# A rotation table for all state-space batches, the gate's token sums in a lane of their own, and new lane paces

## The chip, the cores and the metric

The kernel runs on one core of one Trainium2 chip. Its time is the device time of one execution in microseconds (us). The core's engines each take their instructions in a fixed order and wait for one another by semaphores: TensorE (PE: matmuls, with PEld for its weight loads), VectorE (DVE), ScalarE (ACT), GpSimd (POOL) and SyncE (SP), which here only issues DMA transfers.

## The reference

The reference is one layer of a decoder block with two token mixers side by side, in float32, for 1024 positions and 16 meta tokens put ahead of them, with 1024 features:

```
h     = layer_norm(concat(meta, x))
p     = h @ w_in + b_in            # columns: u_s5 | q | k | v | o | i | f | g_s5 | g_m
z     = gelu(S5(u_s5)) @ w_glu     # S5: 32 groups of 16 channels, 64 complex states each
y_s5  = z[:, :1024] * sigmoid(z[:, 1024:])
y_m   = (sigmoid(o) * head_norm(mLSTM(silu(conv(q)), silu(conv(k)), v, i, f))) @ m_w_out
mix   = sigmoid(g_s5) * y_s5 + sigmoid(g_m) * y_m
h     = layer_norm(ALPHA * h + mix @ w_o)
h     = layer_norm(ALPHA * h + square(relu(h @ w_up + b_up)) @ w_down)
```

The mLSTM is a gated linear attention with four heads; S5 is a linear recurrence per channel group. The output leaves the meta tokens out.

## The kernel before

**Split products.** Every large matrix product is made of three passes on PE: each operand is split into a rounded half (ACT copies it to the rounded type: `whi`, `hT_hi`, `gelh`) and the rest (DVE subtracts: `wlo`, `hT_lo`, `gell`). mm3 (L222 to L228) issues hi x hi (L226), lo x hi (L227) and hi x lo (L228). A product therefore waits for ACT's `whi` (L212, and L1042 in the Strassen part) first and for DVE's `wlo` (L213, L1043) right after.

**Jobs and lanes.** After the first layer norm the projection is cut into jobs of 128 output features, in the order of ORDER: q (queries and keys), v, o, u (the S5 input), g (the S5 gate), m (the other gate), and then z0 to z7 for the GLU product (`z2s`, `sgs`, L944 and L945 add up its parts). Each job loads its weights two jobs ahead, splits them, and runs its matmuls. Everything else is written as Python generators in lanes: `ml` (mLSTM), `cv` (convolution), `s5`, `s5c`, `s5g` (state space), `ah` (the residual and early FFN work). A job that emits matmuls calls pump(dt) with its own length, and each lane then emits its next piece whenever its clock has come; the number that a generator yields is the pause until its next piece. A scheduler turns the emitted program into a fixed order for each engine; PE's work, DVE's, ACT's and the DMA queue are then run in that order, each instruction waiting for its operands and for its tile's slot. Nearly all tiles come from one ring of 30 slots of 4 KB per partition (`slot`).

**State space.** s5_pre (L579) computes the discretised constants for all groups; it is added to lane `s5c` at job S5_START. Then, for each of four batches of 8 groups, s5_consts (L674) makes the batch's matrices (`s5P`, `s5Mi`, `s5Kt`, `s5Rr`, `s5Ri`, `s5Mx`; POOL copies blocks by small DMAs) and its rotation table `s5T`, powers 0 to 129 of a complex rotation for 4 columns, built by doubling: eight levels of six DVE operations (cmul, L572 to L577). s5_batch (L790) uses them: products `s5z` and `s5y` on PE, rotations `s5w` on DVE, and s5_gelu (L866) applies the gelu (`gelf`, `gelh`, `gell`). The tables ML, NL, C5, K5, Z5, D5, W5 and Y5 hold the pauses of these generators for each of the four heads or batches.

**Early residual and FFN work.** ah_scale (L1369) scales the residual rows. up_early (L1400) prepares the first three (PRE) pairs of FFN weight blocks for the later Winograd product: for each pair it loads two blocks (`wur`), makes four sums (`wus`, L1394 to L1397), splits seven blocks (`wpre`, L1412 on ACT and L1413 on DVE), and stores each to memory (`wu_dr`, L1414). Both are added to lane `ah` at job g4.

**The gates and the mLSTM output.** Next to the m gate and the mLSTM output product comes the class Seven: seven Strassen products over blocks of weights and of tokens. The token blocks are `rawb`, loaded by raw_block, and the sums of token blocks are made by sub (L1000 to L1002). begin() loads four blocks at job z7; after the last job all lanes are drained, and first() splits the first weights and makes the sums:

```
for l in lanes.values():
    l.drain()
first()
run7()
```

After that come the output projection with its layer norm, the FFN up and down products and the tail. They aren't touched.

Of the kernel before, what the change touches and what calls it, by code (L numbers as in the profile page):

```python
# [9 lines left out]
F32 = mybir.dt.float32  # L10
F32R = mybir.dt.float32r
I32 = mybir.dt.int32
AF = mybir.ActivationFunctionType
OP = mybir.AluOpType
P = 128
# [4 lines left out]
META = 16  # L20
# [20 lines left out]
ORDER = "q0 q1 v0 q2 v1 q3 o1 o0 v2 o2 o3 u0 u1 v3 u2 g0 u3 g1 o4 o5 o7 o6 g2 g3 g5 g6 g4 g7 m0 m1"  # L41
S5_START = "u0"
NM = 2
SPLIT_UP = 200
PRE = 3
ZD = 1
ML = [2.4, 1.2, 1.68, 4.8]
NL = [0.88, 1.75, 1.75, 1.75]
C5 = [0.7, 0.98, 1.96, 0.49]
K5 = [1.7, 3.4, 1.7, 1.7]  # L50
Z5 = [1.0, 1.0, 1.0, 1.0]
D5 = [2.88, 1.22, 1.44, 1.44]
W5 = [2.21, 1.56, 2.6, 2.6]
Y5 = [1.97, 2.82, 3.38, 2.82]
AFT = 0
VAFT = 2
LOAD0 = "x0 x1 w0 c0 x2 w1 c1 x3 x4 w2 x5 w3 x6"
# [55 lines left out]
def decoder_block(  # L113
# [4 lines left out]
    nc = tc.nc  # L118
    v_, a_, g_, t_ = nc.vector, nc.scalar, nc.gpsimd, nc.tensor
# [9 lines left out]
    def slot(name, dt=F32):  # L129
        return big.tile([P, SLOT], dt, tag="s", name=name)  # L130
# [12 lines left out]

    lanes = {"ml": Lane(), "cv": Lane(), "s5": Lane(), "s5c": Lane(), "s5g": Lane(), "ah": Lane()}
    clock = [0.0]
# [48 lines left out]
    def load_w(job):  # L194
        job.raw = []
        for src, n in job.loads:
            r = slot("wraw") if ring[0] is None else ring[0].tile([P, 1024], F32, tag="wr", bufs=3, name="wraw")
            nc.sync.dma_start(r[:, :n], src)
            job.raw.append(r)
# [379 lines left out]
    def s5_pre():  # L579
# [14 lines left out]
        S5["ni"] = mid.tile([P, 16], I32, name="s5_ni")  # L594
        yield 1.3
        lr, li = lam[:, 0], lam[:, 1]
# [5 lines left out]
        acc_exp(ea, a, (t1, t2))  # L602
        yield 1.3
        r8 = t16("r8")
# [11 lines left out]
        a_.activation(cs, t1, AF.Sin, scale=-1.0, bias=hpi_t[:, 0:1])  # L616
        yield 1.3
        es = slot("s5E")
# [12 lines left out]
        for _ in range(3):  # L631
# [3 lines left out]
            v_.tensor_tensor(p8[:, 0], t1, t2, op=OP.subtract)  # L635
        yield 1.3
        for n in (1, 2, 4):
# [4 lines left out]
                 E[:, 0, n:n + 1].to_broadcast(sh), E[:, 1, n:n + 1].to_broadcast(sh), w1, w2)  # L642
        yield 1.3
        for j in range(8):
# [14 lines left out]
        v_.tensor_tensor(wi, wi, inv, op=OP.mult)  # L659
        yield 1.3  # L660
        sh = [P, 16, 16]

        def v3(ap):
# [5 lines left out]
             v3(tm[:, 0:256]), v3(tm[:, 256:512]))  # L669
        yield 1.3  # L670

    GEL = {}

    def s5_consts(b):  # L674
# [85 lines left out]
        yield K5[b]  # L760
        T = slot("s5T")
        tc_, ts_ = (T[:, i * 520:(i + 1) * 520].rearrange("p (q c) -> p q c", q=4) for i in range(2))
        tmp = slot("s5tt")
        g_.memset(tc_[:, :, 0], 1.0)
        g_.memset(ts_[:, :, 0], 0.0)
        g_.tensor_copy(tc_[:, :, 1], S5["p8"][:, 0, q0:q0 + 4])
        g_.tensor_copy(ts_[:, :, 1], S5["p8"][:, 1, q0:q0 + 4])
        yield C5[b]
        n = 1
        while n < 129:  # L770
            m = min(n, 129 - n)
            sh = [P, 4, m]
            w1 = tmp[:, 0:4 * m].rearrange("p (q c) -> p q c", q=4)
            w2 = tmp[:, 512:512 + 4 * m].rearrange("p (q c) -> p q c", q=4)
            cmul(v_, tc_[:, :, n + 1:n + 1 + m], ts_[:, :, n + 1:n + 1 + m], tc_[:, :, 1:m + 1], ts_[:, :, 1:m + 1],
                 tc_[:, :, n:n + 1].to_broadcast(sh), ts_[:, :, n:n + 1].to_broadcast(sh), w1, w2)
            n *= 2
            yield C5[b]
        S5["m", b] = (RS, Mi, Mx, T)

# [204 lines left out]

    def raw_block(dr, kh, ch, off=0):
        ts = [slot("rawb"), slot("rawb")]
        for i in range(2):
            k = 4 * kh + 2 * i
            c = off + 512 * ch  # L990
            tc.keep_in_program_order(nc.sync.dma_start(s3(ts[i]), dr[k:k + 2, :, c:c + 512].rearrange("k p s -> p k s")))  # L991
        return ts
# [7 lines left out]
    def sub(dst, a, b):  # L1000
        for i in range(2):
            v_.tensor_tensor(dst[i][:, :1024], a[i][:, :1024], b[i][:, :1024], op=OP.subtract)  # L1002

    class Seven:
# [8 lines left out]
        def load(self, i):  # L1013
            if i >= self.ntile():
                return
            r = ring[0].tile([P, 1024], F32, tag="wr", bufs=3, name="wraw")
            for j, (n, p) in enumerate(self.units[2 * i:2 * i + 2]):
                s = {5: 0, 6: 1, 7: 2, 3: 3}.get(n)
                if s is None:
                    t = self.w[self.i0 + 2 * p + (n == 4)].rearrange("p k f -> p (k f)")  # L1020
                    a = t[:, 0:512] if n == 1 else t[:, 512:1024]
                else:
                    a = ws_dr[self.p0 + p, s]
                tc.keep_in_program_order(nc.sync.dma_start(r[:, j * 512:j * 512 + 512], a))
            self.raw[i] = r
# [117 lines left out]
    def gates_and_output():  # L1143
        h00, h10, h01, h11 = home(0, 0), home(1, 0), home(0, 1), home(1, 1)
        g = Seven(3, wf, JGM + NM, 0, {1: h00, 2: h10, 6: h01, 7: h00, 4: h10, 5: h01, 3: h11})
        y = Seven(4, wmo, 0, 3, {1: h00, 2: h10, 6: h01, 7: h11, 4: h00, 5: h10, 3: h01})
        R, M = {}, {}

        def begin():
            for nm, kh, ch in (("12", 0, 1), ("22", 1, 1), ("11", 0, 0), ("21", 1, 0)):  # L1150
                R[nm] = raw_block(h_dr, kh, ch, META)

        def first():
            for i in range(3):
                g.load(i)
            g.split(0)
            sub(R["22"], R["12"], R["22"])
            sub(R["12"], R["12"], R["11"])
            sub(R["11"], R["11"], R["22"])
            to_home(R["11"], h01)  # L1160
            sub(R["21"], R["21"], R["11"])
            R.pop("11")

        def hm_load():
            for nm, kh, ch in (("11", 0, 0), ("12", 0, 1), ("22", 1, 1), ("21", 1, 0)):
                M[nm] = raw_block(hm_dr, kh, ch)

        def y_start():
            for i in range(3):
                y.load(i)  # L1170
            y.split(0)
        ghooks = {1: [lambda: to_home(R.pop("22"), h00)],
                  2: [lambda: to_home(R.pop("21"), h10)],
                  6: [lambda: to_home(R.pop("12"), h01), hm_load],
                  7: [lambda: to_home(M["11"], h00), lambda: sub(M["12"], M["12"], M["22"])],
                  4: [lambda: to_home(M["21"], h10), lambda: sub(M["11"], M["11"], M["12"])],
                  5: [lambda: to_home(M["11"], h01), lambda: sub(M["21"], M["21"], M["11"]), y_start],
                  3: [lambda: to_home(M.pop("12"), h11), lambda: sub(M["11"], M["22"], M["11"])]}
        yhooks = {1: [lambda: to_home(M.pop("21"), h00)],
                  2: [lambda: to_home(M.pop("11"), h10)],  # L1180
                  6: [lambda: to_home(M.pop("22"), h01)],
                  7: [lambda: wo_block(1, 1)],
                  4: [lambda: wo_block(0, 0)],
                  5: [lambda: wo_block(1, 0)],
                  3: [lambda: wo_block(0, 1)]}

        def run():
            g.run(lambda c, p: sdps() if c == "b" else mmps(), gate_evac, ghooks)
            y.run(lambda c, p: sdps() if c == "b" and p else mmps(), ym_evac, yhooks)
        return begin, first, run  # L1190

# [177 lines left out]
    def ah_scale():  # L1369
# [4 lines left out]
        for t in range(9):  # L1374
# [10 lines left out]
            for i, op in enumerate((OP.mult, OP.add)):  # L1385
                v_.tensor_tensor(r[:, :D], r[:, :D], gb[i][:, :D], op=op)
                yield 1.5
            nc.sync.dma_start(ah_dr[(t - 1) * P:t * P, :], r[:, :D])
# [11 lines left out]
    def up_early():  # L1400
        for p in range(PRE):
# [7 lines left out]
            for n, w in ((1, a11), (2, a12), (3, n2[:, 0:512]), (4, a22), (5, n1[:, 0:512]), (6, n1[:, 512:1024]),  # L1409
# [4 lines left out]
                nc.sync.dma_start(wu_dr[p, n - 1], f32(o[:, 0:1024]))  # L1414
                yield 0.9

# [50 lines left out]
    next(ws)  # L1467
    begin, first, run7 = gates_and_output()

    for i, j in enumerate(jobs):  # L1470
# [9 lines left out]
        if j.tag == S5_START:  # L1480
            lanes["s5c"].add(s5_pre())
        if j.tag and j.tag[0] == "o":
            while int(j.tag[1:]) not in HMREADY:
                lanes["cv"].drain()
                lanes["ml"].step()
        if j.tag == "g4":
            lanes["ah"].add(ah_scale())
            lanes["ah"].add(up_early())
        if j.tag == "z7":
            mid_ctx.close()  # L1490
            ring_ctx = ExitStack()
            ring[0] = ring_ctx.enter_context(tc.tile_pool(name="ring", bufs=1, side="left"))
            begin()
        if i >= 5 and i % 2 and ws:
# [583 lines left out]
```

## Time and profile before

| | |
|---|---|
| median of 3 runs | 1549.32 us (1548.83 to 1549.41) |
| the profiled execution | 1548.64 us |
| its span in the trace | 1546.8 us |
| mean granted PE clock | 0.988 |
| PE busy | 1508.0 us, 97% |
| DVE busy | 1080.9 us, 70% |
| ACT busy | 643.8 us, 42% |
| POOL busy | 97.7 us, 6% |

The profile is one execution. Its span runs from the first to the last instruction, and the execution's own time is 1.8 us longer. A row of a view names line, engine, operation, the tile that is written and those that are read; the number of the buffer is left out. An arrow to the left names what ended a wait. PE is nearly always busy, so what matters is the short list of places at which it is not, and the stretches in which its clock was granted at half rate.

### The profile page before, as it was taken

The numbers are of one execution on the slowest core, as the hardware profiler recorded it, in microseconds if no ns is written. First come the engines' busy times: TensorE is split into PE (matmuls) and PEld (weight loads), VectorE is DVE, ScalarE is ACT, GpSimd is POOL, SyncE is SP. The second block draws the span as 40 slices with busy tenths as digits, with TensorE's granted clock in tenths as the row PEclk, the third lists the DMA queues.
The fourth block names the chain that finished last, engine by engine and source line by source line (L and its number), as shares of the span: only waits on it lengthen the run. The fifth ranks groups of instructions, "written<-read, shape, count | busy, mean of one in ns | idle before, by whom it ended". The sixth has DMA issues, their size and how long they took to land.

```text
span 1546.8 us, 20543 instructions
## 1 busy us (share of the span) xinstructions
PE 1508.0 (97%) x7593; PEld 1275.0 (82%) x7593; DVE 1080.9 (70%) x2083; ACT 643.8 (42%) x982; POOL 97.7 (6%) x195
## 2 busy tenths in 40 slices
PE   8999999997999999989999999999999999999996
PEld 8999998996878888868788887888888888888886
DVE  7677555659767865659688675766666689767785
ACT  6524444334354443435543243444444534433430
POOL 0000001124021200000000001000000000000000
PEclk9999999998999999999999999999999999999998
DMA  8513224413354677756272238544443897767642
GB/s 314 166 53 95 67 73 136 117 49 91 117 118 115 172 258 232 283 192 224 82 241 72 83 110 275 176 149 148 150 147 134 275 383 283 242 223 236 201 175 96
DMA packets 122149, 261.19 MB, mean 169 GB/s; under 512 B 14568, under 2 KB 36784, under 8 KB 122048
## 3 DMA queue, kind: packets, MB, share of 16 engines
q1 hardware_dynamic: 111344, 233.00, 44.1%
q0 software_dynamic: 10704, 26.88, 7.3%
q8 instruction: 60, 0.98, 0.3%
q14 instruction: 41, 0.34, 0.1%
HBM read 188.78 MB, written 84.55 MB: 177 GB/s over the span
## 4 chain that ended last, share of the span: by engine, by line
PE 30%; issue 24%; DMA 2%; DVE 1%; SPq 0%; POOL 0%; ACT 0%; POOLq 0%; DVEq 0%
PE mm L228 7%; PE mm L227 7%; PE mm L226 7%; PE sd L227 3%; PE sd L226 3%; PE sd L228 3%; DMA wpre<-wu_dr 1%; DMA rawb<-h_dr 1%; DVE wlo L1043 0%; SPq L991 0%; DMA woraw<-in_wo_dram 0%; POOL wpre L1621 0%; DVE hT_lo L1141 0%; DVE yp L1121 0%; DVE rawb L1002 0%
## 5 line engine op out<-in xcount | busy, mean ns | idle before, releaser
L226 PE MATMUL mm<-hT_hi,whi 128*128 128x512 f32 (+3 forms) x604 | 230.2, 381 | 6.3 <-ACT whi L1042 3.8
L228 PE MATMUL mm<-hT_hi,wlo 128*128 128x512 f32 (+3 forms) x604 | 226.6, 380 | 6.3 <-DVE wlo L213 3.8
L227 PE MATMUL mm<-hT_lo,whi 128*128 128x512 f32 (+3 forms) x604 | 228.4, 378 | 0.0
L228 PEld LDWEIGHTS mm<-hT_hi,wlo 128*128 128x128 f32 x604 | 114.9, 190 | 25.8 <-DVE wlo L213 4.2
L226 PEld LDWEIGHTS mm<-hT_hi,whi 128*128 128x128 f32 x604 | 115.2, 191 | 24.6 <-ACT whi L1042 4.6
L227 PEld LDWEIGHTS mm<-hT_lo,whi 128*128 128x128 f32 x604 | 115.1, 191 | 17.6 <-issue 0.4
L1777 ACT ACTIVATE dwh<-wdr 128x1024 fp32r<-128x1024 f32 x56 | 58.9, 1054 | 86.6 <-DMA wdr<-in_wdn_dram 31.0
L227 PE MATMUL sd<-dwl,dah 128*128 128x512 f32 x240 | 94.5, 394 | 0.0
L228 PE MATMUL sd<-dwh,dal 128*128 128x512 f32 x240 | 94.4, 394 | 0.0
L226 PE MATMUL sd<-dwh,dah 128*128 128x512 f32 x240 | 94.2, 393 | 0.0
L1773 ACT ACTIVATE dah<-da 128x1024 fp32r<-128x1024 f32 x56 | 58.7, 1052 | 83.6 <-PE sd L227 37.1
L1774 DVE TENSOR_TENSOR dal<-da,dah 128x1024 fp32r<-128x1024 f32 x56 | 68.2, 1219 | 24.0 <-ACT dah L1773 23.5
L228 PE MATMUL mm<-dwh,dal 128*128 128x512 f32 (+1 forms) x224 | 84.5, 378 | 0.0
L226 PE MATMUL mm<-dwh,dah 128*128 128x512 f32 (+1 forms) x224 | 84.4, 377 | 0.0
L227 PE MATMUL mm<-dwl,dah 128*128 128x512 f32 (+1 forms) x224 | 84.3, 377 | 0.0
L1778 DVE TENSOR_TENSOR dwl<-wdr,dwh 128x1024 fp32r<-128x1024 f32 x56 | 68.2, 1219 | 12.7 <-ACT dwh L1777 11.9
L213 DVE TENSOR_TENSOR wlo<-wraw,whi 128x1024 fp32r<-128x1024 f32 (+1 forms) x46 | 56.1, 1221 | 26.7 <-ACT whi L212 20.8
L226 PE MATMUL mm<-whi,hT_hi 128*128 128x256 f32 (+1 forms) x256 | 74.3, 290 | 0.0
L228 PE MATMUL mm<-whi,hT_lo 128*128 128x256 f32 (+1 forms) x256 | 74.0, 289 | 0.0
L227 PE MATMUL mm<-wlo,hT_hi 128*128 128x256 f32 (+1 forms) x256 | 73.0, 285 | 0.0
L228 PE MATMUL mm<-th,wul 128*128 128x512 f32 x156 | 61.6, 395 | 0.0
L227 PE MATMUL mm<-tl,wuh 128*128 128x512 f32 x156 | 61.5, 394 | 0.0
(474 smaller groups left out, 3688.0 us busy)
## 6 DMA issues: line engine op xcount, KB each, us to landing
da<-act_dr SPq DMA_DIRECT2D x56, 512.0 KB, 5.5
wdr<-in_wdn_dram SPq DMA_DIRECT2D x56, 512.0 KB, 6.7
wur<-in_wup_dram SPq DMA_DIRECT2D x32, 512.0 KB, 4.4
act_dr<-upy SPq DMA_DIRECT2D x64, 256.0 KB, 2.5
wraw<-in_wf_dram SPq DMA_DIRECT2D x30, 512.0 KB, 5.3
wu_dr<-wpre SPq DMA_DIRECT2D x21, 512.0 KB, 4.9
wpre<-wu_dr POOLq DMA_DIRECT2D x21, 512.0 KB, 5.1
act_dr<-upx SPq DMA_DIRECT2D x32, 256.0 KB, 3.1
```

What stands on the lines that cost most here:

```text
L213: todo.append(lambda e=v_, r=r, hi=hi, lo=lo, n=n: e.tensor_tensor(lo[:, :n], r[:, :n], f32(hi[:, :n]), op=OP.subtract))
L226: t_.matmul(ps, ah, bh, start=(i == 0 and part[0]), stop=False, skip_group_check=skip)
L227: t_.matmul(ps, ah, bl, start=False, stop=False, skip_group_check=skip)
L228: t_.matmul(ps, al, bh, start=False, stop=(i == n - 1 and part[1]), skip_group_check=skip)
L1773: a_.activation(ah[:, :D], a[:, :D], AF.Copy)
L1774: v_.tensor_tensor(alo[:, :D], a[:, :D], f32(ah[:, :D]), op=OP.subtract)
L1777: a_.activation(wh, raw[i], AF.Copy)
L1778: v_.tensor_tensor(wl, raw[i], f32(wh), op=OP.subtract)
```

## The change

- The rotation table is built once, for all 16 columns and 66 powers, by a new generator s5_table that follows s5_pre in lane `s5c`. For each batch s5_consts copies its four columns (two ACT copies) and makes the powers 66 to 129 by one cmul of six DVE operations.
- s5_pre and the table start at job o3 instead of u0, and the pauses of nearly all S5 and mLSTM generators are new.
- The gate's token sums are a generator, token_sums, in a new lane `gp`, added at job z2; three of the four blocks are loaded there. The middle pool is closed and the ring pool opened at z1 instead of z7, with one more buffer for weights and two for tokens. begin() at z7 drains that lane and loads the fourth block; early() at z6 loads the first three gate weights; first() makes only the last sum.
- ah_scale and up_early are added at job m1 instead of g4, with pauses of 4 instead of 1.5 and 2.75 instead of 0.9.
- load_w takes its tiles from the general ring always, and the scratch of the software DMA ring is set to 4096.

The order of the jobs (ORDER) and all of PE's products are the same. The core of the diff, with the changed tables cut to two lines:

```diff
-S5_START = "u0"
+S5_START = "o3"
...
-C5 = [0.7, 0.98, 1.96, 0.49]
+C5 = [0.94, 0.98, 2.09, 1.32]
...
+AH_START = "m1"
+AHY = 4
+UPY = 2.75
+PRY = 3.25
+TBY = 2.2
+GY = 8.0
+GS = 4.0
...
+    def s5_table():
+        S5["T"] = T = mid.tile([P, 2, 16, 66], F32, name="s5_T")
+        tm, (c, s) = slot("s5tt"), (T[:, 0], T[:, 1])
...
+        yield TBY
+        n = 1
+        while n < 65:
+            m = min(n, 65 - n)
+            sh = [P, 16, m]
+            cmul(v_, c[:, :, n + 1:n + 1 + m], s[:, :, n + 1:n + 1 + m], c[:, :, 1:m + 1], s[:, :, 1:m + 1],
+                 c[:, :, n:n + 1].to_broadcast(sh), s[:, :, n:n + 1].to_broadcast(sh),
+                 *(tm[:, i * 512:i * 512 + 16 * m].rearrange("p (q c) -> p q c", q=16) for i in range(2)))
+            n *= 2
+            yield TBY
...
+        t1, s1 = S5["T"][:, 0, q0:q0 + 4], S5["T"][:, 1, q0:q0 + 4]
...
+        a_.activation(tc_[:, :, 0:66], t1, AF.Copy)
+        a_.activation(ts_[:, :, 0:66], s1, AF.Copy)
+        sh = [P, 4, 64]
+        cmul(v_, tc_[:, :, 66:130], ts_[:, :, 66:130], t1[:, :, 2:66], s1[:, :, 2:66],
...
         yield C5[b]
-        n = 1
-        while n < 129:
-            m = min(n, 129 - n)
...
-            n *= 2
-            yield C5[b]
...
+        def token_sums():
+            R["12"], R["22"] = raw_block(h_dr, 0, 1, META), raw_block(h_dr, 1, 1, META)
+            R["11"] = raw_block(h_dr, 0, 0, META, True)
+            yield GY
+            yield from sub(R["22"], R["12"], R["22"])
+            yield from sub(R["12"], R["12"], R["11"])
+            yield from sub(R["11"], R["11"], R["22"])
+            to_home(R["11"], h01)
...
-                yield 1.5
+                yield AHY
...
-                yield 0.9
+                yield UPY
...
+            lanes["s5c"].add(s5_table())
...
-        if j.tag == "g4":
+        if j.tag == AH_START:
             lanes["ah"].add(ah_scale())
             lanes["ah"].add(up_early())
-        if j.tag == "z7":
+        if j.tag == "z1":
             mid_ctx.close()
...
+        if j.tag == "z2":
+            lanes["gp"].add(token_sums())
+        if j.tag == "z6":
+            early()
+        if j.tag == "z7":
             begin()
...
-    nc = _bacc.Bacc("TRN2", target_bir_lowering=False, num_devices=1)
+    nc = _bacc.Bacc("TRN2", target_bir_lowering=False, num_devices=1, dynamic_dma_scratch_size=4096)
```

In the changed kernel the lines have moved: whi and wlo are L219 and L220 (L1064 and L1065 in the Strassen part), mm3's passes L233 to L235, up_early's sums L1423 to L1426, its halves L1441 and L1442 and its stores L1443.

## What was predicted, before the changed kernel ran

> **What bounds the kernel now.** I read the page's busy row first, then TensorE's waits, then the clock by stretch, then single places in the timeline.
>
> ```profile
> span 1546.8 us, 20543 instructions
> PE 1508.0 (97%) x7593; PEld 1275.0 (82%) x7593; DVE 1080.9 (70%) x2083; ACT 643.8 (42%) x982; POOL 97.7 (6%) x195
> ```
>
> PE is the bound, so the change can only fill PE's waits or open new ones. The waits (line, releaser: us in total, times, longest):
>
> ```profile
> PE mm L228 <- DVE wlo L213: 3.8, 1, 3.8
> PE mm L226 <- ACT whi L1042: 3.8, 1, 3.8
> ...
> PE s5k L741 <- DVE s5Ri L719: 2.9, 1, 2.9
> PE mm L228 <- DVE wlo L1043: 2.4, 1, 2.4
> PE pt L513 <- DVE hraw L506: 1.7, 1, 1.7
> ...
> PE mm L226 <- DVE v L354: 1.3, 1, 1.3
> PE mm L226 <- ACT whi L212: 1.2, 1, 1.2
> PE s5y L858 <- DVE s5w L846: 1.2, 1, 1.2
> ```
>
> Eight waits, each met once, make 18.3 us; nearly all of them name a half of a weight (whi, wlo) or a state-space tile that ACT or DVE finished late. The columns of the next view are the stretch, its length, each engine's busy time with its instructions, and at the end the granted clock, the DMA share and GB/s.
>
> ```profile
> 350.00:400.00 50.00, 42.11 (x232) 36.77 (x231) 45.92 (x152) 21.72 (x35) 19.93 (x23) 0.90 0.44 128
> 650.00:700.00 50.00, 43.86 (x180) 34.59 (x179) 32.05 (x34) 19.84 (x25) 0.00 (x0) 0.93 0.62 220
> ```
>
> At 350 to 400 DVE is full (45.9 of 50), and s5Ri, whi L212 and wlo L213 make 2.9 + 1.2 + 3.8 = 7.9 us of waits there, with 1.3 (v) just ahead. The clock of 0.90 means 0.10 x 50 x 2 = 10 us at half rate. At 650 to 700, between the last z job and the first gate product, PE waits 3.8 + 2.4 = 6.2 us.
>
> **One table (gain).** The lines of the rotation table in before (count, ns min/median/max):
>
> ```profile
> L572 DVE TENSOR_TENSOR s5tt<-s5T x32: 145/180/426, 340.6 to 518.7; 128x4 f32<-128x4 f32 x8, 128x8 f32<-128x8 f32 x4, 128x16 f32<-128x16 f32 x4, 128x32 f32<-128x32 f32 x4
> L577 DVE TENSOR_TENSOR s5T<-s5tt x32: 153/184/425, 351.0 to 521.3; 128x4 f32<-128x4 f32 x8, 128x8 f32<-128x8 f32 x4, 128x16 f32<-128x16 f32 x4, 128x32 f32<-128x32 f32 x4
> ```
>
> Six such lines of 32 are 192 small DVE operations; 42 for the one table plus 4 x 6 of 128x256 replace them. More than the number, the place counts: the preamble and the table start at o3, so batch 0 no longer builds its table (48 operations) in the full stretch. I book the 1.3 + 7.9 = 9.2 us of waits as gone. Of the 10 us at half rate at least 10 - 7.9 = 2 were work (1 us lost), at most all (5 lost); I take 3, since the 0.90 stands for stalls and work mixed. Gain 12.2 (9.2 to 14.2). What is late next there would be the mLSTM chain (hraw L506, 1.7), which I leave as it is. s5y's 1.2 wait goes too, since its s5w stood behind batch 3's table.
>
> **A new wait on ACT (loss).** ACT in the changed kernel, at the end of the last o job and the product after it (whi is the rounded half of that product's weights, gelf the gelu of batch 2's output):
>
> ```order
> L521 ACTIVATE hmF<-pt,mngt 128x512 x2
> L878 ACTIVATE s5Y<-s5y 128x512
> L891 ACT_TABLE_LOAD
> L891 ACTIVATE gelf<-s5yc 128x8x128
> L894 ACTIVATE gelh<-gelf 128x1024
> L878 ACTIVATE s5Y<-s5y 128x512
> L789 ACTIVATE s5T<-s_T 128x4x66
> L790 ACTIVATE s5T<-s_T 128x4x66
> L905 ACT_TABLE_LOAD
> L905 ACTIVATE osig<-mm,bft 128x512 x2
> L219 ACTIVATE whi<-wraw 128x1024
> ```
>
> In before this gelu stood at the same stage of the work, but the two hmF ahead of it had a whi of their own right behind them, and hraw of the mLSTM chain stood between; ACT's rows there:
>
> ```order
> L874 ACT_TABLE_LOAD
> L874 ACTIVATE gelf<-s5yc 128x8x128
> L888 ACT_TABLE_LOAD
> L888 ACTIVATE osig<-mm,bft 128x512
> L496 ACTIVATE hraw<-pn,dd 128x256
> L877 ACTIVATE gelh<-gelf 128x1024
> L496 ACTIVATE hraw<-pn,dd 128x256
> L212 ACTIVATE whi<-wraw 128x1024
> ```
>
> What moved: both hmF, which can only start once PE has done its transposes (pt), now stand with the gelu, two table loads and the o gate (osig) in one row, and the next product's whi is last of it. The prices, from ACT's timeline (start, us) and three rows by group (mean ns after the bar):
>
> ```profile
> 422.70 0.59 ACT L734 ACTIVATE s5Mi<-s5p 128x512 f32<-128x512 f32 x1
> 423.31 1.28 ACT L874 ACT_TABLE_LOAD   x1
> 424.60 2.25 ACT L874 ACTIVATE gelf<-s5yc 128x1024 f32<-128x1024 f32 x1
> 426.89 1.06 ACT L877 ACTIVATE gelh<-gelf 128x1024 fp32r<-128x1024 f32 x1
> ...
> 430.11 1.27 ACT L888 ACTIVATE osig<-mm,bft 128x512 f32<-128x512 f32 x2
> ```
> ```profile
> L212 ACT ACTIVATE whi<-wraw 128x1024 fp32r<-128x1024 f32 (+1 forms) x46 | 48.2, 1054 | 4.2 <-DMA wu_dr<-wpre 1.9 <-PE s5y L857 1.4 <-DMA wraw<-in_wf_dram 0.5
> L514 ACT ACTIVATE hmF<-pt,mngt 128x512 f32<-128x512 f32 x16 | 10.5, 686 | 7.7 <-PE pt L513 7.6
> L812 ACT ACTIVATE s5Z<-s5z 64x130 f32<-64x130 f32 x32 | 8.3, 270 | 27.9 <-PE s5z L802 20.5 <-DVE s5Z L810 7.0
> ```
> ```profile
> L857 PE MATMUL s5y<-s5U,s5Mx x64: 271/275/582, 363.7 to 554.3; 128*128 128x128 f32 x64
> ```
>
> Sum: hmF 2 x 0.69, s5Y 2 x 0.59 (as s5Mi), loads 2 x 1.28, gelf 2.25, gelh 1.06, two copies of 128x264 at 0.35 (no row has them; between 0.27 of s5Z and 0.59), osig 1.27, whi 1.05 = 11.5 us (11.3 to 12.0). PE has 15 small matmuls between those transposes and the product, at most 0.275 each, 4.1 us. So whi is 7.4 us late; wlo follows on DVE 1.2 after it, behind the gates' multiplies, and PE has 0.9 us of work in hand: 1.5 more. With half a clock after it (1.7, about half of what the three waits above cost), 10.6 (0 if something I don't see covers it, to 13).
> The Trainium skill, "ScalarE: Activation LUTs", What ACT_TABLE_LOAD costs, puts a switch at 1.28 us and a drain of 1.38 beside it. The trace has no such drain: ACT ends s5Mi at 423.29, loads at 423.31 and starts gelf at 424.60. By the page two switches would add 2.8 us to this wait, and the forecast would be 1572.5.
>
> **The drain before the first gate product (loss).** up_early makes the weight sums of three FFN pairs: per pair 4 DVE sums, 7 ACT copies, 7 DVE differences (wpre), 7 stores. In before it starts at g4 and is done before z7. Now ah_scale starts at m1 with paces of 4, up_early follows it in the same lane, and the loop that drains all lanes stands in the code ahead of first(). DVE in before, up to the first gate product's wlo (L1043):
>
> ```order
> L944 TENSOR_TENSOR z2s<-mm,z2s 128x512
> L1002 TENSOR_TENSOR rawb<-rawb 128x1024
> L998 TENSOR_TENSOR hT_lo<-rawb,hT_hi 128x2x512
> L1002 TENSOR_TENSOR rawb<-rawb 128x1024
> L945 TENSOR_TENSOR sgs<-z2s,sgs 128x512
> L1043 TENSOR_TENSOR wlo<-wraw,whi 128x1024
> ```
>
> DVE now, the end of the same stretch: the third pair, after the last z2s, one sgs and two such pairs (of the first pair's sums, the four already stood ahead of that z2s):
>
> ```order
> L1423 TENSOR_TENSOR wus<-wur 128x512
> L1424 TENSOR_TENSOR wus<-wus,wur 128x512
> L1425 TENSOR_TENSOR wur<-wur 128x512
> L1426 TENSOR_TENSOR wus<-wur,wus 128x512
> L1442 TENSOR_TENSOR wpre<-wur,wpre 128x512 x2
> L1442 TENSOR_TENSOR wpre<-wus,wpre 128x512
> L1442 TENSOR_TENSOR wpre<-wur,wpre 128x512
> L1442 TENSOR_TENSOR wpre<-wus,wpre 128x512 x2
> L1442 TENSOR_TENSOR wpre<-wur,wpre 128x512
> L1065 TENSOR_TENSOR wlo<-wraw,whi 128x1024 x2
> ```
>
> SP's queue at the same place (wur is an FFN pair's weights coming in, wu_dr their halves going out):
>
> ```order
> L1433 DMA wur<-in_wup_dram 128x1024 x2
> L1443 DMA wu_dr<-wpre 128x1024 x10
> L1433 DMA wur<-in_wup_dram 128x1024
> L1443 DMA wu_dr<-wpre 128x1024 x3
> L1433 DMA wur<-in_wup_dram 128x1024
> ```
>
> What moved: the token sums (rawb) are gone from here but for the last, 21 differences and 8 sums stand in their place, and the third pair's loads stand behind 13 stores. The rows for it, DVE's timeline and the DMA rate in two full stretches:
>
> ```profile
> 671.84 0.69 DVE L944 TENSOR_TENSOR z2s<-mm,z2s 128x512 f32<-128x512 f32 x1
> 672.44 1.21 DVE L1002 TENSOR_TENSOR rawb<-rawb 128x1024 f32<-128x1024 f32 x1
> ...
> 675.84 0.68 DVE L945 TENSOR_TENSOR sgs<-z2s,sgs 128x512 f32<-128x512 f32 x1
> 676.44 1.22 DVE L1043 TENSOR_TENSOR wlo<-wraw,whi 128x1024 fp32r<-128x1024 f32 x1
> ```
> ```profile
> 650.00:653.00 3.00, 3.00 (x15) 2.44 (x14) 2.88 (x5) 2.58 (x4) 0.00 (x0) 1.00 1.02 404
> 659.00:662.00 3.00, 3.00 (x15) 2.42 (x14) 1.32 (x2) 0.35 (x1) 0.00 (x0) 1.00 0.98 311
> ```
> ```profile
> 669.56 0.40 PE L228 MATMUL mm<-gelh,wlo 128*128 128x512 f32 x1
> ```
>
> By DVE alone: a 128x512 operation follows another every 0.60 us (671.84 to 672.44). PE ends z7 at 669.96; z2s, sgs, 21 + 8 pieces are 31 x 0.60 = 18.6, so with 0.9 of pieces still ahead wlo starts near 689.5 and not at 676.4: 13 us more. By the transfers: from z7's end, when the second pair's slots come free, 17 transfers of 0.524 MB (2 + 10 + 1 + 3 + 1) must pass before the third pair is in: 8.9 MB at 404 GB/s is 22.1 us, at 311 it is 28.7. Then 11 pieces (6.7) and wlo (1.2): 669.96 + 22.1 + 7.9 = 700.0 against wlo's end at 677.7, 22.3 more. I take that, since the 404 belongs to a stretch of these very stores; bounds 13 and 29. With some 1 us of clock more than now (0.93 above already pays a half rate), 23.3.
> The Trainium skill, "DMA: Bandwidth & Descriptors", Where 436 GB/s comes from, says that the HBM side binds near 358 GB/s. The trace shows 404 over 3 us. By the page the 17 transfers take 24.9, and the sum would be 1572.8.
>
> **The rest at nothing.** Token sums in z2 to z5: four subtractions stand ahead of one wlo in z5, 0 to 2, I take 0.5. The three gate weights loaded a job earlier, the larger ring: hidden by z6. The smaller software-DMA scratch concerns POOL, 6% busy: 0, up to 4 if a full queue holds batch 0's blocks.
>
> **Sum**, against the profiled execution's own 1548.64 (0.7 under the median of 1549.32, so I read it as the same): 1548.6 - 12.2 - 1.2 + 10.6 + 23.3 + 0.5 = 1569.6, say 1570.
>
> **Rivals.** (1) DVE, not the transfers, ends the drain: stores overlap better than two full stretches show. Then 9.3 less, 1560. For: the stores' slots, some ten, free early. Against: third-pair loads behind 13 stores. (2) The gelu block is covered on ACT: 1559. For: in before none of the four gelus made PE wait. (3) Faster: the engines run ahead at the queue heads, so that the drain and the gelu block are done before PE arrives. It decides at the last z jobs: DVE would have to finish the third pair by 657 of PE's time; then only the gains and the 0.5 are left, 1536. Against: the z2s rows wait for PE and DVE keeps its order. (4) The table wasn't what filled 350 to 400, and the same waits come from other work: 1570 + 12 = 1582. For: DVE holds also mLSTM and s5Ri there.
>
> **Numbers.** Forecast 0.50, (1) 0.22, (2) 0.10, (3) 0.07, (4) and slower transfers (+6.4, 1576) 0.11. Range 1557 to 1581: it takes in (1), (2) and the slow transfers, and leaves out (3) and most of (4). A measurement of this kernel tells some 0.2%, 3.1 us, from no change. Faster 0.07; same 0.03, where (1), (2) and a full 14.2 of gain come together; slower 0.90.
>
> **What would show it.** Right: the waits on s5Ri, v and s5w gone; a wait of some 9 us on whi L219 and wlo L220 near the last o job; a wait of nearly 29 us on whi L1064 and wlo L1065 in all, with wpre L1442 on DVE through it, DMA share near 1 and third-pair loads landing late. Wrong: wpre between z jobs, or PE's wait before the first gate product at 7 us or less.

## The result and the profile after

The changed kernel takes 1574.01 us (median of 4 runs, 1572.51 to 1576.88) against 1549.37 for the kernel before beside it, a ratio of 1.0161 (95% interval 1.0143 to 1.0179): 1.6% slower. The forecast was 1570 with a range of 1557 to 1581. The profiled execution took 1573.8 us; the head of its page:

```profile
span 1572.0 us, 20419 instructions
PE 1507.7 (96%) x7593; PEld 1274.6 (81%) x7593; DVE 1065.7 (68%) x1957; ACT 645.0 (41%) x989; POOL 85.0 (5%) x183
```

PE's work is what it was (1508.0 before), so the 25.2 us that the span has grown by are waits and half clock. TensorE's waits in the changed kernel (total, times, longest):

```profile
PE mm L233 <- ACT whi L1064: 33.4, 1, 33.4
PE mm L233 <- ACT whi L219: 5.6, 3, 3.1
PE s5z L819 <- ACT s5Y L878: 3.0, 1, 3.0
...
PE mm L235 <- DVE wlo L220: 2.7, 2, 2.2
PE pt L520 <- DVE hraw L513: 2.3, 1, 2.3
...
PE s5y L874 <- ACT hmF L521: 0.4, 1, 0.4
```

The waits on v, s5Ri and s5w are gone. One wait of 33.4 us, on the weights of the first gate product, has taken their place, and behind it stand small ones on ACT.

To see where time comes and goes, take the same PE instruction in both traces and subtract its start times. Four such places: a product early in the z jobs, the last product of z7, the fifth matmul of the first gate product, and the last store of the output. Before:

```profile
596.01 0.62 PE L228 MATMUL mm<-gelh,wlo 128*128 128x512 f32 x2
...
677.71 0.80 PE L228 MATMUL mm<-hT_hi,wlo 128*128 128x512 f32 x1 [2.36 <-DVE wlo L1043]
```
```profile
1540.69 0.33 SPq L1890 DMA_DIRECT2D out_dram<-arow  x1
```

After:

```profile
591.75 0.62 PE L235 MATMUL mm<-gelh,wlo 128*128 128x512 f32 x2
...
671.76 0.39 PE L235 MATMUL mm<-gelh,wlo 128*128 128x512 f32 x1
...
707.38 0.63 PE L235 MATMUL mm<-hT_hi,wlo 128*128 128x512 f32 x1
```
```profile
1569.25 0.33 SPq L1925 DMA_DIRECT2D out_dram<-arow  x1
```

The changed kernel is 4.3 us ahead early in the z jobs, 2.2 behind at the end of z7 (671.76 against 669.56, the row shown in the prediction), 29.7 behind in the first gate product, 28.6 at the last store, and 25.2 at the end of the span. So the way is -4.3, +6.5, +27.5, -1.1, -3.4. Each stage in turn.

**The state-space stretch, -4.3.** The columns are as in the prediction: stretch, length, busy times, then clock, DMA share, GB/s. After, the stretch that cost most before, the one of the gelu, and one in the z jobs:

```profile
350.00:400.00 50.00, 50.00 (x284) 43.45 (x283) 41.05 (x88) 26.31 (x50) 15.33 (x29) 1.00 0.50 124
450.00:500.00 50.00, 42.95 (x211) 35.09 (x210) 32.98 (x71) 28.95 (x45) 10.68 (x18) 0.90 0.52 127
600.00:650.00 50.00, 45.51 (x189) 36.30 (x189) 30.07 (x33) 10.91 (x14) 0.00 (x0) 0.97 0.44 158
```

At 350 to 400 PE has no gap, the clock is full and DVE has 41.05 us of work instead of 45.92. At 450 to 500 it is the other way round. There ACT's timeline in the changed kernel has the row of work that the order had shown:

```profile
461.06 1.26 ACT L521 ACTIVATE hmF<-pt,mngt 128x512 f32<-128x512 f32 x2 [5.25 <-PE pt L520]
462.21 0.60 ACT L878 ACTIVATE s5Y<-s5y 128x512 f32<-128x512 f32 x1
462.82 1.28 ACT L891 ACT_TABLE_LOAD   x1
464.12 2.04 ACT L891 ACTIVATE gelf<-s5yc 128x1024 f32<-128x1024 f32 x1
...
468.37 1.28 ACT L905 ACT_TABLE_LOAD   x1
...
470.82 1.05 ACT L219 ACTIVATE whi<-wraw 128x1024 fp32r<-128x1024 f32 x1
```

From hmF to the end of whi it is 10.8 us without a gap. PE waits for s5Y (3.0), whi (3.1), wlo (0.5 of the 2.7 above) and hmF (0.4), 7.0 in all. The clock of 0.90 is 10 us at half rate, of which the 3.6 for whi and wlo are idle anyway; half of the other 6.4 is lost. That makes 10.2 for the block, and with 4.3 us won in all, the one table and the rest of this stretch gained 14.5.

**The z jobs, +6.5.** Two of the small waits are here, 2.3 on whi and 2.2 on wlo, and half of the 3 us at half rate (0.97 of 50): 6.0 of the 6.5. The token loads in SP's queue, and a stretch of 8 us:

```profile
591.19 9.68 SPq L1008 DMA_DIRECT2D rawb<-h_dr  x6
```
```profile
592.00:600.00 8.00, 8.00 (x36) 6.53 (x35) 5.54 (x7) 2.14 (x3) 0.00 (x0) 1.00 1.06 252
```

DVE's timeline behind them:

```profile
605.04 2.58 DVE L1019 TENSOR_TENSOR rawb<-rawb 128x1024 f32<-128x1024 f32 x2 [4.45 <-DMA rawb<-h_dr]
...
614.36 1.21 DVE L1019 TENSOR_TENSOR rawb<-rawb 128x1024 f32<-128x1024 f32 x1
615.49 1.22 DVE L220 TENSOR_TENSOR wlo<-wraw,whi 128x1024 fp32r<-128x1024 f32 x1
```

then ACT, and PE:

```profile
610.40 1.06 ACT L1014 ACTIVATE hT_hi<-rawb 128x1024 fp32r<-128x1024 f32 x1 [5.17 <-DVE rawb L1019]
611.37 1.04 ACT L219 ACTIVATE whi<-wraw 128x1024 fp32r<-128x1024 f32 x1
```
```profile
612.46 0.50 PE L233 MATMUL mm<-gelh,whi 128*128 128x512 f32 x1 [2.32 <-ACT whi L219]
...
616.77 0.50 PE L235 MATMUL mm<-gelh,wlo 128*128 128x512 f32 x1 [2.18 <-DVE wlo L220]
```

Read it backwards. PE waits for whi; whi stands on ACT behind hT_hi of a token block; hT_hi waits for DVE's sums; and DVE's first sum waited 4.45 us for the token blocks, six loads that SP issued between 591.2 and 600.9. Two things made them land late. SP itself waited ahead of three of the loads, 3.4 us twice and 1.5 us once, each time for an instruction of PE or DVE to end. And the DMA engines were full (share 1.06) at only 252 GB/s: beside the loads, a transfer of 1 MB that POOL had issued at 588.1 (ws_dr, sums of later weights; the kernel before has it at the same stage) was under way until 602.6. How much each of the two cost isn't shown.

**The drain before the first gate product, +27.5.** The changed kernel from the end of z7 to DVE's start on the third pair, and three stretches within it:

```profile
672.16:699.14 26.98, 0.00 (x0) 0.00 (x0) 15.35 (x26) 7.83 (x14) 0.00 (x0) 0.58 0.93 349
677.50:690.00 12.50, 0.00 (x0) 0.00 (x0) 10.01 (x17) 4.65 (x9) 0.00 (x0) 0.50 1.02 402
690.00:692.50 2.50, 0.00 (x0) 0.00 (x0) 0.00 (x0) 0.00 (x0) 0.00 (x0) 0.50 0.96 287
692.50:698.50 6.00, 0.00 (x0) 0.00 (x0) 0.00 (x0) 1.15 (x2) 0.00 (x0) 0.50 1.03 408
```

PE is idle in all of it. DVE works for 15.35 us and is idle in the last 11.6, with the DMA engines full or nearly so until 698.5. What DVE waits for is in its timeline, and why that is late in SP's:

```profile
699.14 0.69 DVE L1423 TENSOR_TENSOR wus<-wur 128x512 f32<-128x512 f32 x1 [11.59 <-DMA wur<-in_wup_dram]
...
705.89 1.22 DVE L1065 TENSOR_TENSOR wlo<-wraw,whi 128x1024 fp32r<-128x1024 f32 x1
```
```profile
676.61 10.45 SPq L1443 DMA_DIRECT2D wu_dr<-wpre  x10
687.11 1.24 SPq L1433 DMA_DIRECT2D wur<-in_wup_dram  x1
688.44 3.56 SPq L1443 DMA_DIRECT2D wu_dr<-wpre  x3
692.04 1.24 SPq L1433 DMA_DIRECT2D wur<-in_wup_dram  x1
```

Ten stores stand ahead of the third pair's first load and three more ahead of its second. That one is issued at 692.0, DVE gets its pair at 699.1, and 11 pieces later the gate's wlo can run. The queue isn't full from the start: the second pair is loaded as z7 ends, and the first store is issued only at 676.6.

**The end, -3.4.** At the end of the program every engine has a few instructions called DRAIN, and POOL's longest takes up most of the time behind the last store. POOL's, grouped by line (ns min/median/max), before and then after:

```profile
L2074 POOLq DRAIN  x3: 46/97/6502, 1539.5 to 1546.5; - x3
```
```profile
L2109 POOLq DRAIN  x3: 46/98/2988, 1568.0 to 1571.8; - x3
```

The longest of the three went from 6.50 to 2.99 us, 3.5 less.

### The profile page after: what moved, and what is told of

The parts are those of the page before. It is cut to its first block, busy times and chain, and to the rows that moved or that the text cites. A ratio compares the mean times of both kernels' runs of the same rounds, so it can differ in the third digit from the quotient of the medians.

```text
span 1572.0 us, 20419 instructions
## 1 busy us (share of the span) xinstructions
PE 1507.7 (96%) x7593; PEld 1274.6 (81%) x7593; DVE 1065.7 (68%) x1957; ACT 645.0 (41%) x989; POOL 85.0 (5%) x183
## 4 chain that ended last, share of the span: by engine, by line
PE 75%; issue 16%; DMA 3%; DVE 3%; ACT 2%; SPq 0%; POOLq 0%; DVEq 0%; ACTq 0%
PE mm L235 18%; PE mm L233 18%; PE mm L234 18%; PE sd L234 3%; PE sd L233 3%; PE sd L235 3%; PE mm L1334 2%; PE mm L1342 1%; PE pu L484 1%; PE pn L481 1%; PE pn L480 1%; DMA wur<-in_wup_dram 1%; DMA wiB<-wrow_dr 1%; DMA rawb<-h_dr 1%; PE ln L1290 0%
## 5 line engine op out<-in xcount | busy, mean ns | idle before, releaser
L233 PE MATMUL mm<-hT_hi,whi 128*128 128x512 f32 (+3 forms) x604 | 232.4, 385 | 36.7 <-ACT whi L1064 33.4
L235 PE MATMUL mm<-hT_hi,wlo 128*128 128x512 f32 (+3 forms) x604 | 226.5, 378 | 0.5 <-DVE wlo L220 0.5
L233 PEld LDWEIGHTS mm<-hT_hi,whi 128*128 128x128 f32 x604 | 115.0, 190 | 56.3 <-ACT whi L1064 34.2
L235 PEld LDWEIGHTS mm<-hT_hi,wlo 128*128 128x128 f32 x604 | 114.6, 190 | 20.0 <-DVE wlo L220 1.5
L235 PE MATMUL sd<-dwh,dal 128*128 128x512 f32 x240 | 94.3, 394 | 0.0
L233 PE MATMUL sd<-dwh,dah 128*128 128x512 f32 x240 | 94.1, 393 | 0.0
L235 PE MATMUL mm<-dwh,dal 128*128 128x512 f32 (+1 forms) x224 | 84.5, 378 | 0.0
L233 PE MATMUL mm<-dwh,dah 128*128 128x512 f32 (+1 forms) x224 | 84.4, 378 | 0.0
L220 DVE TENSOR_TENSOR wlo<-wraw,whi 128x1024 fp32r<-128x1024 f32 (+1 forms) x46 | 56.3, 1227 | 27.9 <-ACT whi L219 21.0
L233 PE MATMUL mm<-whi,hT_hi 128*128 128x256 f32 (+1 forms) x256 | 74.6, 291 | 0.0
L235 PE MATMUL mm<-whi,hT_lo 128*128 128x256 f32 (+1 forms) x256 | 73.4, 287 | 0.0
L235 PE MATMUL mm<-th,wul 128*128 128x512 f32 x156 | 61.5, 394 | 0.0
```

The lines of the kernel that those rows point to most:

```text
L220: todo.append(lambda e=v_, r=r, hi=hi, lo=lo, n=n: e.tensor_tensor(lo[:, :n], r[:, :n], f32(hi[:, :n]), op=OP.subtract))
L233: t_.matmul(ps, ah, bh, start=(i == 0 and part[0]), stop=False, skip_group_check=skip)
L235: t_.matmul(ps, al, bh, start=False, stop=(i == n - 1 and part[1]), skip_group_check=skip)
```

## The experiments

The theory: three things cost (the drain of up_early, the gelu block on ACT, the token sums in z) and three gain (one table, the shorter end, gate weights loaded early), and they add up. The rivals are that the table was not what freed the stretch at 350 to 400, that the drain is not up_early's doing, and that the price of each place depends on the others. Ratios are against the kernel before, run on the same chip, with 95% intervals.

**The residual and FFN lane early again.** In the changed kernel:

```diff
-AH_START = "m1"
-AHY = 4
-UPY = 2.75
+AH_START = "g4"
+AHY = 1.5
+UPY = 0.9
```

> The changed kernel with only the residual and early FFN work put back: added at g4, pauses 1.5 and 0.9 as before. Theory (the drain of up_early makes the 33.4 us wait before the first gate product): that wait falls to 7 us or less, the z jobs get some waits of 2 to 3 us because up_early's pieces now share DVE and the DMA queue with the token sums, and the time is 1547 to 1551. Rival (the wait comes from the token sums, the gate weights' early loads or the ring pool opened at z1): 1570 to 1574, the wait stays.

Measured: 1561.62 us, 1.008 (1.0065 to 1.0095). The wait on whi L1064 is gone, and yet only 12 of the 27 us come back. PE's waits say why:

```profile
PE mm L233 <- ACT whi L219: 19.9, 6, 6.9
```

Five of the six waits on whi and two of the three on wlo, together 19 us, lie between 615 and 682, in the z jobs: up_early's loads and stores now share SP's queue and the DMA engines with the token loads. ACT's row at the longest, and ACT's largest sum of waits from 610 to 690:

```profile
651.15 1.06 ACT L219 ACTIVATE whi<-wraw 128x1024 fp32r<-128x1024 f32 x1 [2.93 <-DMA wu_dr<-wpre]
```
```profile
ACT wpre L1441 <- DMA wu_dr<-wpre: 12.8, 6, 6.4
```

Here the weights' copy itself waits for a store of up_early to land; elsewhere wpre copies do, 12.8 us in six waits, and hold up what stands behind them on ACT. These tiles come from the one ring, so the likely reason is that each store has to free a slot. So the drain was up_early's, as both said, but the token sums in z2 to z5 cost far more once up_early is there too. Neither theory nor rival had this.

**The lane late, alone, in the kernel before.** Start at m1, pauses 4 and 2.75; nothing else:

```diff
-        if j.tag == "g4":
+        if j.tag == "m1":
...
-                yield 1.5
+                yield 4
...
-                yield 0.9
+                yield 2.75
```

> The kernel before with one part of the change alone: residual and early FFN work added at m1 with pauses 4 and 2.75. Theory: the drain stands before the first gate product here too, now with all token sums behind it and eight token loads in the same queue: wait 6.2 + 27 to 38, time 1576 to 1587. Rival (that part needs the rest of the change to hurt): 1549 to 1553.

Measured: 1590.35 us, 1.0267 (1.0253 to 1.0281), 41 us more, above what was expected. In DVE's timeline:

```profile
701.51 0.69 DVE L1394 TENSOR_TENSOR wus<-wur 128x512 f32<-128x512 f32 x1 [9.59 <-DMA wur<-in_wup_dram]
...
718.78 1.22 DVE L1043 TENSOR_TENSOR wlo<-wraw,whi 128x1024 fp32r<-128x1024 f32 x1 [10.43 <-ACT whi L1042]
```

and in SP's:

```profile
711.39 4.51 SPq L1024 DMA_DIRECT2D wraw<-in_wf_dram  x6
```

The same wait for the third pair is there. Behind it comes a second one, of 10.4 us: here the gate's own weights (wraw) are issued after the last store. In the changed kernel they are loaded at z6 and this part is missing. So the late lane alone makes the loss at this place, and the early gate weights, which the prediction put at nothing, take some of it back.

**The loads ahead of the stores.** In the changed kernel up_early issues its six loads first, with the order of all else kept:

```diff
+        rr = [[slot("wur"), slot("wur")] for _ in range(PRE)]
         for p in range(PRE):
-            r = [slot("wur"), slot("wur")]
             for j in range(2):
-                nc.sync.dma_start(r[j][:, :D], wup[2 * p + j].rearrange("p k f -> p (k f)"))
+                nc.sync.dma_start(rr[p][j][:, :D], wup[2 * p + j].rearrange("p k f -> p (k f)"))
+        for p in range(PRE):
+            r = rr[p]
```

> The changed kernel with up_early's six weight loads issued ahead of its stores; work and all else as they are. Theory (the drain waits for transfers, the third pair's loads behind 13 stores): DVE's 11.6 us of idle in the drain goes, the wait falls from 33.4 to 20 to 23, time 1562 to 1565. Rival (DVE's work alone sets the drain's length, 18.6 us and more): nothing changes, 1574.

Measured: 1562.48 us, 1.0085 (1.007 to 1.0099), and the wait on whi L1064 is 21.0 instead of 33.4. The drain by stretches:

```profile
676.00:684.00 8.00, 0.00 (x0) 0.00 (x0) 8.00 (x15) 4.80 (x10) 0.00 (x0) 0.50 0.97 389
684.00:692.00 8.00, 0.00 (x0) 0.00 (x0) 8.00 (x15) 5.29 (x11) 0.00 (x0) 0.50 1.03 408
```

DVE no longer waits. The kernel is 11.5 us faster, which fits the 11.59 that DVE had stood idle for the third pair, and what is left is DVE's own work. This was rival (1) of the prediction (1560), and it takes a change in the order of issue to make it true.

**The token sums back at z7.** In the changed kernel:

```diff
         def begin():
+            lanes["gp"].add(token_sums())
             lanes["gp"].drain()
...
-        if j.tag == "z2":
-            lanes["gp"].add(token_sums())
```

> The changed kernel with the token-sum lane added at z7 instead of z2, so that its loads and subtractions come where they came before. Theory (the waits of 2.3 and 2.2 us on whi and wlo in the z jobs come from subtractions that wait for token loads, with a weight half queued behind them): both go, 6 us with the clock; the token loads and sums now join the drain, whose wait grows from 33.4 towards the 47 that the kernel before had with the late drain: 1576 to 1583. Rival (the z waits come from the residual rows' traffic): they stay, 1582 to 1589.

Measured: 1572.07 us, 1.0148 (1.0131 to 1.0165). The z waits are gone (600 to 650 has a clock of 1.00 and PE busy 50.00), and the wait on whi L1064 grows by only 2.2, to 35.6: the drain waits for transfers and not for DVE, so most of the sums find room. The expectation had them added in full, which was too much. Beside the kernel before with its lane late (a wait of 47.0, the same token sums at z7), the 35.6 also suggest what loading the gate's weights at z6 is worth there: some 11 us. (The two kernels differ in their state-space work too, so this is an estimate.)

**Both.** The early lane and the sums at z7 in one kernel.

> The changed kernel with both put back: early FFN work at g4 with the pauses of before, token sums at z7. What is left of the change is the one table, the earlier start, the new pauses and the scratch. Theory: 1549.4 - 3.3 (end) - 13.1 (waits at 340 to 380 gone) - 1.2 + 10.3 (gelu block on ACT) + 0 to 2 = 1542 to 1544, no wait over 3 us in the z jobs, and 6 to 8 before the first gate product. Rival (the ring pool, moved to z1, or the weights loaded early cost by themselves): 1550 or more.

Measured: 1535.98 us, 0.9915 (0.99 to 0.993), 0.85% faster than before and better than expected. At the boundary only this is left:

```profile
PE mm L235 <- DVE wlo L1065: 2.6, 2, 2.0
```

with the clock at 1.00 from 650 to 700. The gate's weights have been loaded since z6, and ACT has made whi by 658.6, before z7 ends. The expectation had left 6 to 8 us of waits here; that only 2.6 remain, without half clock, is a good part of what it was too high by. Of the 13.9 us won against the kernel before, 3.3 are the scratch's (below). The lane early alone was worth 12.4 us in the changed kernel and the sums at z7 alone 1.9; together they are worth 38. With the lane early, moving the sums out of z2 to z5 gives 25.6 us (1561.62 to 1535.98), with the lane late 1.9. The two places are not independent: up_early and the token sums collide wherever both lie in the z jobs.

**And the gelu four units of its lane's clock earlier.** On top of that kernel, for all four batches:

```diff
-        yield 14.0
+        yield 10.0
         gf = slot("gelf")
```

> As e7_ah_early_sums_z7, with the pause ahead of the gelu cut from 14 to 10, by which the gelu and its table loads no longer stand between hmF and the next product's whi. Theory (the wait near 466 is that block on ACT): the waits on s5Y and whi there fall from 3.0 + 3.1 to about 3 in all, and with the clock the time is 5 to 8 lower than e7, 1535 to 1539. Rival (hmF and the o gate alone make whi late): within 2 of e7.

Measured: 1531.6 us, 0.9888 (0.9873 to 0.9902), the fastest of all, 1.1% faster than the kernel before; 4.4 us less than the kernel it was built on, where 5 to 8 were expected. ACT's timeline at the same place:

```profile
466.72 1.28 ACT L905 ACT_TABLE_LOAD   x1
...
469.17 1.05 ACT L219 ACTIVATE whi<-wraw 128x1024 fp32r<-128x1024 f32 x1
```

gelf and gelh are out of the row, and so the wait on s5Y is gone; but the table load that leads back to the sigmoid stayed, and so did a wait of 2.3 us on whi. In all the waits of this block fall from 7.0 to 3.5 (whi 2.3, wlo 0.8, hmF 0.4), and the clock from 450 to 500 is 1.00 instead of 0.90.

**The scratch alone.** In the kernel before, only the scratch of the software DMA ring:

```diff
-    nc = _bacc.Bacc("TRN2", target_bir_lowering=False, num_devices=1)
+    nc = _bacc.Bacc("TRN2", target_bir_lowering=False, num_devices=1, dynamic_dma_scratch_size=4096)
```

> The kernel before with only the software-DMA scratch of 4096. The last transfer is issued 28.57 us later in the changed kernel, but its span is only 25.25 us longer, so 3.3 us went at the very end. Theory (a smaller scratch makes the end of the program shorter): all of the body as before, the end 3.3 us shorter, 1546. Rival (the end varies by itself, or by when it falls): 1549.3, no change.

Measured: 1546.11 us (11 runs), 0.998 (0.9971 to 0.9989), 3.3 us less. Its closing row:

```profile
L2074 POOLq DRAIN  x3: 46/98/2908, 1540.8 to 1544.5; - x3
```

**Which part freed the stretch at 350 to 400.** Three kernels, each with one part of the change put back in the one with lane early and sums at z7 (1535.98 us). First, preamble and table start at u0, as in before:

```diff
-S5_START = "o3"
+S5_START = "u0"
```

> As e7_ah_early_sums_z7, but the preamble and the table start at u0 as before. My step (the place counts: the table must be built ahead of the full stretch): the waits at 340 to 380 come back for the most part, 9 to 13 us, 1551 to 1557. Rival (the number counts: 66 operations in the place of 192): no wait there, but the mLSTM chain near 440 is later by some 5 us and the gelu block by some 5 us less late, 1541 to 1546.

Measured: 1540.79 us, 0.9946 (0.993 to 0.9962). No wait came back at 350 to 400: the start at u0 costs 4.8 us elsewhere. That is the rival's side, the number and not the place. Of the 4.8 the waits show 2.4 more on hraw (4.7 in two) and a new one of 1.4 on dd, both in the mLSTM, and 1.1 more on whi, while the 3.0 on s5Y is gone; the rest isn't assigned.

Second, the one table, with the start and all S5 and mLSTM pauses of before:

> As e7_ah_early_sums_z7, but with S5_START and all pauses of before: what is left of the change is the one table, the scratch and the gate weights loaded a job earlier. Theory (fewer DVE operations end the waits at 338 to 380): no wait on s5Ri, no 3.8 on wlo there, something of 3 to 7 us near 320 to 340 and near 470, 1535 to 1542. Rival (the new pauses did it): the 7.9 us of waits at 350 to 400 are still there, 1546 to 1552.

Measured: 1535.05 us, 0.9909 (0.9893 to 0.9926). The waits are gone here too, and the new start and paces add nothing that can be told from it (1535.98). So the start at u0 costs its 4.8 us only beside the new pauses.

Third, the new start and pauses, with the four eight-level tables of before:

> As e7_ah_early_sums_z7, but with the four tables built in eight levels per batch as before: the early start and the new pauses without the one table. Theory (fewer operations): DVE's work is only moved, waits of 3 to 4 us each turn up near 420, 447 and 580, 1539 to 1546. Rival (the early start and the pauses alone are enough): 1534 to 1537.

Measured: 1551.73 us (10 runs), 1.0018 (1.0008 to 1.0029), outside both expectations. Nothing waits at 340 to 400 in this kernel either, but there is a wait that none of the others has, and ACT shows what it is for:

```profile
PE mm L233 <- ACT gelh L902: 14.4, 1, 14.4
```
```profile
597.09 1.28 ACT L899 ACT_TABLE_LOAD   x1 [10.21 <-DMA s5yc<-ys_dr]
```

The longer pauses of C5 are now taken nine times in each batch instead of once, and the last batch's gelu comes after PE has reached the z product. So the time is no clean trial of the pauses; it shows only that with these values they can't be had without the table. The stretch at 340 to 400 is a trial, though: the early start and the pauses free it without the table, as the table frees it without them.

## Why the prediction was right, and where its steps were not

The forecast was 1569.6 for the profiled execution, 4.2 below the 1573.8 that it took, on the side it named, and the largest term, the drain, is there for the reason it named. That it came so near is in part luck: it missed 10.2 us of loss (6.0 in the z jobs, 4.2 in the drain) and 6.0 us of gain, which hides more than half of that. Term by term:

| step | booked | measured |
|---|---|---|
| waits and clock at 350 to 400, and s5w | -13.4 | none of these waits left, clock 1.00; -14.5 with all else up to the z jobs |
| gelu block on ACT | +10.6 | +10.2 |
| token sums in z | +0.5 | +6.5 |
| drain before the first gate product | +23.3 | +27.5 |
| scratch, end of the program | 0 | -3.4 |
| first gate product to the last store | 0 | -1.1 |

**One table.** The waits are gone as booked, and rival (4) falls; the size, 14.5, is what remains when the gelu block is taken off, and holds whatever else changed up to the z jobs. What isn't borne out is the sentence that the place counts more than the number: with the start back at u0 the waits stay away, and the early start without the one table keeps them away too, so either is enough for this stretch. What was named as late next there, hraw, is 2.3 instead of 1.7 and of no weight.

**The gelu block.** The row was put at 11.5 us and took 10.8; the price of the row was right, and the kernel with the gelu earlier took back 4.4 us by taking gelf and gelh out of it. The make-up of the cost was another: 8.9 us of waits on whi and wlo and 1.7 of clock were booked (the 1.5 for wlo isn't worked out by the numbers beside it, 1.2 less 0.9 is 0.3, and 0.5 was measured); the runs have 3.6 on whi and wlo, 3.4 ahead of them on s5Y and hmF, which the prediction didn't name, and 3.2 of clock. That the sums meet, 10.6 and 10.2, is luck in part. The prediction set the rule of the Trainium skill, "ScalarE: Activation LUTs", What ACT_TABLE_LOAD costs, of a drain beside a load, against rows without one. The changed kernel has none either: s5Y ends at 462.81, the load starts at 462.82 and gelf at 464.12. (With its 2.8 us more the prediction's own sum comes to 1572.4, not 1572.5.)

**The drain.** The mechanism was right: third-pair loads behind 13 stores, DVE idle for them. The size was too small by 4 us, and the term that was mis-sized is the transfers: 22.1 us from z7's end to the third pair, where 27.0 were measured (672.2 to 699.1). The work behind them took 8.0 (to wlo's end at 707.1) where 7.9 were booked, and of the 1 us of clock only 0.2 is in the 27.5. The rate was right: where transfers were under way without a pause they moved 402 GB/s over 12.5 us and 408 over 6.0, against the 404 taken. What the sum left out is that the queue has pauses. It has the second pair alone until the first halves are made and the first store goes out at 676.6; it dips to 287 from 690.0 to 692.5; and it has hardly anything to move between 698.5 and the start of DVE. So the mean is 349, over which 9.4 MB passed and not 8.9. The lower bound on the rate, 311, covered this without being the reason (its case comes to 6.6 us more, not the 6.4 that the prediction has). The rule of the Trainium skill, "DMA: Bandwidth & Descriptors", Where 436 GB/s comes from, that the HBM side binds near 358 GB/s, would seem to fit the mean of 349, but the 402 and 408 within it go beyond, as do 403 over the same 12.5 us in the kernel with the loads first; so here it is no ceiling, and the rows decide. The section works the figure out as half of a stack's rate for two cores, and this kernel runs on one. (With its 24.9 us in place of 22.1 the prediction's own sum comes to 1572.4, not 1572.8.)

**The token sums in z.** This is the step that was wrong: 0.5 against 6.5. It asked only what stands ahead of one wlo on DVE. It didn't ask when the sums' own operands come (six loads beside POOL's transfer, 4.45 us of DVE's time), nor what stands behind them on ACT: hT_hi, which waits for the sums, and the product's whi behind hT_hi. With up_early beside it the same step cost 25.6.

**The rest at nothing.** The early gate weights were no nothing: with the lane late they spare a second wait, of 10.4 us in the kernel with the late lane alone. The scratch was put at 0 to 4 lost and gained 3.4; it was not read from the end of the program, where the trace of before had the 6.50.

The losses of 27.5 and 6.5 can be had back by four lines of the schedule, and part of the gelu's by a fifth. What is then left of the change makes the kernel 0.85% and 1.1% faster than before.

What stays open: whether the new pauses do anything for the time without the table, since the kernel that was to show it ran into its own last gelu; and what the 1.1 us won after the first gate product are due to.

## What to carry to other kernels

Work that a lane has not emitted by a drain point stands, in code order, in front of what comes next, on every queue; its price here was its own work and, on top of it, the time for which that work stood idle for loads behind stores (11.6 us). So issue the loads first, and ask of every lane put later what it will be drained in front of. When work is moved into a quiet stretch, follow its operands back to the transfer and its engine queues forward to the next thing that PE needs: an instruction that waits on ACT stops the whole queue behind it. And try moved pieces together as well as one by one: here one of two pieces cost 1.9 us where the other was late and 25.6 where they met.

## What the runs showed of the hardware

- The scratch of the software DMA ring is paid at the end of the program: POOL's closing DRAIN took 6.50 us before, and 2.99 and 2.91 with a scratch of 4096; the time follows (3.3 us in the kernel with nothing else changed).
- Transfers of 512 KB from one queue moved 402 GB/s over 12.5 us and 408 over 6.0 with stores first and the last loads between them, and 403 over the same 12.5 us with the loads first. With POOL's 1 MB transfer beside token loads the engines were as full (1.06) at 252.
- In the wait of 33.4 us the clock was granted at half (0.50 from 677.5 on), and it stayed so for the first 5 us of matmuls behind it: 0.63 us each and 0.43 apart, instead of 0.39 and 0.23.
